# A float32r decoder layer on one core: operand tiles moved to other places in SBUF

## The chip, the cores and the metric

The kernel runs on one core of a Trainium2 chip. The metric is device time in microseconds (us). A program on this core issues work to TensorE (PE, and PEld for its weight loads), VectorE (DVE), ScalarE (ACT), GpSimd (POOL) and SyncE (SP, which here issues the DMAs).

## The reference, cut to what matters

One layer of a decoder for 256 prompt tokens and 8 sample tokens (264 columns in all), in float32:

```
h += 1/2 * rms_post(swiglu_1(rms_pre(h)))            # 2048 -> 2 x 5632 -> 2048
u  = rms_pre(h); proj = u @ w_in                      # 2048 -> 10288
mix = concat(conv_group(proj), ssd_group(proj)) @ w_out
h += rms_post(mix)
h += 1/2 * rms_post(swiglu_2(rms_pre(h)))             # as the first
h += rms_post(sigmoid(rms_pre(h) @ w_ple_gate) * (p @ w_ple_proj))
```

Nearly all arithmetic is in the products with the weight matrices.

## The kernel before, in words

Activations stand with features on the 128 partitions and the 264 tokens along the free dimension. A product with a weight matrix is cut into blocks of 128 x 128 weights; for one block of 128 output features the kernel adds up the blocks of the contraction in one PSUM tile (`acc` or `ps`).

Each float32 product is made of three matmuls in float32r (`mm3`). A weight block is split into a rounded part `hi` and a remainder `lo` (tiles `whi`, `wlo`), and an input tile `act` holds the rounded part of 264 columns (half 0) and the remainder (half 1):

```
nc.tensor.matmul(acc, hi, x[:, 0, :], start=first, stop=False)        # L250
nc.tensor.matmul(acc, hi, x[:, 1, :], start=False, stop=False)        # L251
return nc.tensor.matmul(acc, lo, x[:, 0, :], start=False, stop=last).ins   # L252
```

So L250 and L252 stream half 0 of the input tile past the weights, and L251 streams half 1. Each of the three loads its own 128 x 128 weights.

The weights come in an order written out in a table (`PLAN`). `Weights.load` fetches 8 blocks (512 KB) by a DMA on SP's queue into a tile `wraw` (L153), ACT rounds it into `whi` (L154), DVE subtracts to get `wlo` (L155). Four buffers of each are used in turn. `split` fills an input tile: ACT writes half 0, DVE half 1; 32 buffers `act` are used in turn. `gemm_one` makes one output block, 16 blocks of contraction by three matmuls; `gemm_first` and `gemm_pair` are the same with several output blocks.

Where the tiles lie matters for the change. The built program puts the 32 `act` buffers at byte 23264 of each partition and every 2304 bytes (9 x 256) from there. The four buffers of `wraw` lie from 96992, of `whi` from 113376, of `wlo` from 129760, each 4096 bytes from the last. Counted modulo 256 bytes, half 0 of every `act` tile starts at 224, half 1 (1056 bytes further) at 0, and every block of `whi` and `wlo` at 224. The small tiles (`h`, `tmp`, `y` and so on) lie behind the weight buffers.

`act` tiles are also used twice as plain buffers for DMA: `load_p` reads the input `p` into one (L503), and the projection of `p` is stored from eight of them to `pproj` in HBM (L530), where it is read again near the end.

Of the kernel before, what the change touches and what calls it, by code (L numbers as in the profile page):

```python
# [19 lines left out]
P = 128  # L20
NP_ = 256
NS = 8
T = NP_ + NS
XSTRIDE = 576
DM = 2048
KD = DM // P
FF = 5632
# [100 lines left out]
class Weights:  # L128
# [9 lines left out]
    def load(self, between=()):  # L138

        tc, nc, i = self.tc, self.tc.nc, len(self.done)  # L140
        n = len(PLAN[i][1]) * len(PLAN[i][2])
        src = self.w[i, :, : n * P].rearrange("p (n c) -> p n c", n=n)
        tiles = []
        with nullcontext() if between else tc.high_priority(offset=1000):
            for a in range(0, n, 8):
                if a // 8 < len(between):
                    between[a // 8]()
                m = min(8, n - a)
                raw, hi, lo = (
                    self.pool.tile([P, 8, P], t, tag=tag, bufs=bufs, name=f"{tag}{i}_{a}")[:, :m, :]  # L150
                    for t, tag, bufs in ((F32, "wraw", 4), (F32R, "whi", 4), (F32R, "wlo", 4))
                )
                self.dma = nc.sync.dma_start(raw, src[:, a : a + m, :])  # L153
                nc.scalar.copy(hi, raw)  # L154
                nc.vector.tensor_tensor(out=lo, in0=raw, in1=hi.bitcast(F32), op=ALU.subtract)  # L155
                tiles += [(hi[:, k, :], lo[:, k, :]) for k in range(m)]
        self.done.append(tiles)
# [11 lines left out]
def kernel(ctx: ExitStack, tc: tile.TileContext, a: dict):  # L169
# [13 lines left out]
    uid = [0]  # L183

    def nm(s):
        uid[0] += 1
        return f"{s}_{uid[0]}"
# [7 lines left out]
    def tmp():  # L195
        return apool.tile([P, T], F32, tag="tmp", bufs=6, name=nm("tmp"))

    def act_tile():
        t = xpool.tile([P, XSTRIDE], F32R, tag="act", bufs=32, name=nm("act"))
        return t[:, : 2 * T].rearrange("p (i t) -> p i t", i=2)  # L200

    def ytile():
        return apool.tile([P, T], F32, tag="y", bufs=16, name=nm("y"))
# [4 lines left out]
    def rtile():  # L208
        return apool.tile([P, T], F32, tag="rr", bufs=3, name=nm("rr"))
# [44 lines left out]
    def split(x, gain=None):  # L254

        t = act_tile()
        if gain is None:
            nc.scalar.copy(t[:, 0, :], x)  # L258
            tt(t[:, 1, :], x, t[:, 0, :].bitcast(F32), ALU.subtract)
        else:  # L260
            act(t[:, 0, :], x, AF.Identity, scale=gain)
            stt(t[:, 1, :], x, gain, t[:, 0, :].bitcast(F32), ALU.mult, ALU.subtract)
        return t
# [45 lines left out]
    def rsqrt(out, x, bias=0.0, scale=1.0):  # L309

        act(out, x, AF.Ln, bias=bias, scale=scale)
        act(out, out, AF.Exp, scale=-0.5)

    def rms_scale(p, n):

        r = rtile()
        rsqrt(r, p, eps1, 1.0 / n)
        return r
# [47 lines left out]
    def ffn(xs, sq, done):  # L366
# [5 lines left out]
        def scale(behind):  # L372
            p = sq.total(behind)
            rsqrt(r, p, eps1, 1.0 / DM)
            nc.vector.tensor_scalar(
                out=eq, in0=p, scalar1=EPS / P, scalar2=EPS * EPS * DM / P, op0=ALU.mult, op1=ALU.add
            )
# [42 lines left out]
    def ffn_scale(ysq, eq):  # L420
# [4 lines left out]
        with tc.high_priority():  # L425
            rsqrt(rs, ysq.total(), scale=4.0 / DM)
        return rs
# [73 lines left out]
    def load_p():  # L501
        pt = act_tile().bitcast(F32)
        nc.sync.dma_start(pt, a["p"])  # L503
        pacts.extend(split(pt[:, k, :]) for k in range(2))
# [10 lines left out]
    r = rtile()  # L515
    rsqrt(r, q2, scale=1.0 / DM)


    pproj = dram.tile([P, KD, T], F32, name="pproj")
    for q in range(2):  # L520
        w = ws.next()
        for m in range(8):
            acc = acc_tile()
            mm3(acc, w[m], pacts[0], True, False)
            mm3(acc, w[8 + m], pacts[1], False, True)
            if m % 2 == 0:
                t = act_tile().bitcast(F32)
            nc.scalar.copy(t[:, m % 2, :], acc)
            if m % 2:
                nc.sync.dma_start(pproj[:, 8 * q + m - 1 : 8 * q + m + 1, :], t)  # L530
# [3 lines left out]
    for k in range(KD + 2):  # L534
        if k < KD:
            t = tmp()
            tt(t, ys[k], rs, ALU.mult, nc.gpsimd if k % 2 and k > 2 else nc.vector)
            tt(H(k), H(k), t, ALU.add, nc.gpsimd if k else nc.vector)
        if k >= 2:
            t = tmp()  # L540
# [372 lines left out]
    def update_input(rs, post, pre):  # L913

        xs, sq = [], SumSq(KD, eng=nc.vector)
        for k in range(KD + 2):
            if k < KD:
                with tc.high_priority() if k < 2 else nullcontext():
                    residual(k, ys[k], rs, post)
                    xs.append(split(H(k), V(pre, k)))  # L920
            if k >= 2:
                sq.add(H(k - 2))
        return xs, sq

    with tc.high_priority():
        rs = rms_scale(ysq.total(), DM)
    xs, sq = update_input(rs, "mix_post", "ffn2_pre")
# [48 lines left out]
    for m in range(KD):  # L976
# [6 lines left out]
        t = tmp()  # L983
# [11 lines left out]
    for k in TAIL_TENSOR:  # L995
        p = tps.tile([P, T], F32, tag="sum", bufs=3, name=nm("sum"))
# [22 lines left out]
    for k, n in TAIL_VECTOR:  # L1019
        e, h = pair(e4, k, n), pair(h4, k, n)  # L1020
        on_pe = [i for i in range(k, k + n) if i in TAIL_TENSOR]
        if on_pe:
            tc.keep_in_program_order(tt(e, e, rows(rp, n), ALU.mult))
            for i in on_pe:
                p = sums[TAIL_TENSOR.index(i)]
# [4 lines left out]
        t = tps.tile([P, 2, 512], F32, tag="prod", bufs=1, name=nm("prod"))[:, :n, :T]  # L1030
# [133 lines left out]
```

## Time and profile before

| what | before |
|---|---|
| median of 2 runs | 2432.86 us (2430.39 to 2435.34) |
| the profiled execution: its time | 2432.44 us |
| its span, first to last instruction | 2430.7 us |
| mean granted TensorE clock | 0.993 |
| PE busy | 2367.7 us (97%) |
| DVE, ACT, POOL busy | 1569.2, 1181.4, 298.4 us |
| DMA | 489.89 MB, 202 GB/s in the mean |

The span is 1.7 us shorter than the execution's own time. Busy time of PE counts each matmul from its start to its modelled end, and matmuls overlap; the pace of a stream is therefore read from starts, or from the number of matmuls in a long window. A group's row has the count, the busy time, the mean duration of one in ns, and the idle time ahead of them.

### The profile page before, as it was taken

The page shows a single profiled execution, that of the slowest core. Times are in us where ns is not written, and L with a number is a line of the kernel's source. Part 1 is how long each engine was busy: PE and PEld are TensorE (multiplying, and loading weights), DVE is VectorE, ACT ScalarE, POOL GpSimd, SP SyncE. Part 2 cuts the span into 40 slices and gives each one's busy share as a digit, 9 for nine tenths or more (in the row PEclk, how much of TensorE's full clock was granted, in tenths as well). Part 3 has the DMA queues.
Part 4 walks back from the last instruction along what each step waited for, and adds up shares of the span by engine and source line. Part 5 has one row for each costly group of instructions (what it writes and reads, how often), then busy time and mean ns, then how long its engine had stood idle before and what let it go on. Part 6 is the DMA issues. An engine that isn't in the chain of part 4 may idle for free.

```text
span 2430.7 us, 47409 instructions
## 1 busy us (share of the span) xinstructions
PE 2367.7 (97%) x19448; PEld 2342.7 (96%) x19448; DVE 1569.2 (65%) x2333; ACT 1181.4 (49%) x1771; POOL 298.4 (12%) x295
## 2 busy tenths in 40 slices
PE   8999999999999889999999999999999999999988
PEld 8999999999999889999999999999999999999988
DVE  6554455545557858988798975766545565565585
ACT  6444444433456465665565545544444443344465
POOL 0400000000015212122122010101000000000103
PEclk9999999999999999999999999999999999999999
DMA  7655555555556666666666556476766776676553
GB/s 249 217 183 184 182 183 182 183 183 183 183 169 207 213 180 193 207 216 202 210 216 205 181 181 216 153 238 228 240 213 223 237 236 217 217 236 206 184 191 132
DMA packets 166250, 489.89 MB, mean 202 GB/s; under 512 B 25568, under 2 KB 42640, under 8 KB 166032
## 3 DMA queue, kind: packets, MB, share of 16 engines
q1 hardware_dynamic: 166032, 486.86, 62.0%
q8 instruction: 152, 2.49, 0.4%
q14 instruction: 66, 0.54, 0.1%
HBM read 465.65 MB, written 22.42 MB: 201 GB/s over the span
## 4 chain that ended last, share of the span: by engine, by line
PE 84%; DVE 6%; issue 3%; ACT 3%; DMA 2%; POOL 1%; SPq 0%; ACTq 0%; POOLq 0%; DVEq 0%
PE acc L250 27%; PE acc L251 27%; PE acc L252 27%; DVE wlo L155 2%; DVE y L219 1%; ACT whi L154 1%; PE ps L306 1%; DVE h L216 1%; DMA ab<-d_cs 1%; DMA cbc<-d_bc 1%; DVE ych L794 1%; PE ps L250 0%; ACT tmp L243 0%; DMA d_bc<-rows 0%; PE ps L251 0%
## 5 line engine op out<-in xcount | busy, mean ns | idle before, releaser
L252 PE MATMUL acc<-act,wlo 128*128 128x264 f32 x6224 | 1770.7, 285 | 4.3 <-DVE wlo L155 4.1
L251 PE MATMUL acc<-act,whi 128*128 128x264 f32 x6224 | 1756.6, 283 | 6.3 <-DVE act L216 6.2
L250 PE MATMUL acc<-act,whi 128*128 128x264 f32 x6224 | 1747.7, 283 | 3.4 <-DVE tmp L216 2.1
L155 DVE TENSOR_TENSOR wlo<-wraw,whi 128x1024 fp32r<-128x1024 f32 (+2 forms) x812 | 986.9, 1217 | 597.9 <-ACT whi L154 595.5
L154 ACT CAST whi<-wraw 128x1024 fp32r<-128x1024 f32 (+2 forms) x812 | 829.9, 1026 | 961.9 <-PE acc L251 717.3
L250 PEld LDWEIGHTS acc<-act,whi 128*128 128x128 f32 x6224 | 1175.5, 190 | 6.0 <-issue 2.1
L251 PEld LDWEIGHTS acc<-act,whi 128*128 128x128 f32 x6224 | 1169.2, 188 | 9.9 <-DVE act L216 7.9
L252 PEld LDWEIGHTS acc<-act,wlo 128*128 128x128 f32 x6224 | 1167.9, 188 | 8.3 <-DVE wlo L155 6.4
L216 POOL TENSOR_TENSOR run<-run,tmp 128x264 f32<-128x264 f32 x93 | 87.8, 944 | 962.9 <-ACT tmp L243 961.8
L216 POOL TENSOR_TENSOR s<-s,eap 128x1024 f32<-128x1024 f32 x24 | 48.8, 2035 | 630.4 <-DMA s<-in_hst 630.4
L219 DVE SCALAR_TENSOR_TENSOR y<-v,vec,y 128x251 f32<-128x251 f32 (+23 forms) x240 | 118.1, 512 | 1.2
L219 DVE SCALAR_TENSOR_TENSOR s<-bb,xds,s 128x128 f32<-128x128 f32 x192 | 52.7, 346 | 66.1 <-POOL s L216 66.1
L216 POOL TENSOR_TENSOR h<-h,cbc 128x512 f32<-128x512 f32 x48 | 73.6, 1553 | 166.0 <-DMA cbc<-d_bc 90.9
L258 ACT CAST act<-tmp 128x264 fp32r<-128x264 f32 x120 | 48.7, 410 | 69.9 <-DVE tmp L216 55.2
L216 DVE TENSOR_TENSOR tmp<-acc,rr 128x264 f32<-128x264 f32 x100 | 43.0, 430 | 51.0 <-PE acc L252 50.8
L216 DVE TENSOR_TENSOR tmp<-tmp,acc 128x264 f32<-128x264 f32 x86 | 36.7, 427 | 38.7 <-PE acc L252 38.6
L216 DVE TENSOR_TENSOR act<-tmp,act 128x264 fp32r<-128x264 f32 x120 | 56.1, 471 | 0.3
L243 ACT ACTIVATE tmp<-tmp 128x264 f32<-128x264 f32 x112 | 47.0, 420 | 8.7 <-DVE tmp L216 8.4
L243 ACT ACTIVATE tmp<-y 128x264 f32<-128x264 f32 x67 | 28.0, 425 | 44.1 <-DVE y L216 43.0
L216 DVE TENSOR_TENSOR y<-y,acc 128x264 f32<-128x264 f32 x80 | 34.0, 425 | 24.0 <-PE acc L252 24.0
L794 DVE TENSOR_REDUCE ych<-h 128x4 f32<-128x512 f32 x48 | 32.4, 678 | 17.5 <-POOL h L216 17.5
L250 PE MATMUL ps<-act,whi 128*128 128x264 f32 x96 | 28.4, 304 | 15.4 <-ACT whi L154 8.1
(165 smaller groups left out, 926.1 us busy)
## 6 DMA issues: line engine op xcount, KB each, us to landing
wraw<-in_w SPq DMA_DIRECT2D x756, 512.0 KB, 4.7
h<-in_hst SPq DMA_DIRECT2D x48, 256.0 KB, 3.9
s<-in_hst SPq DMA_DIRECT2D x24, 512.0 KB, 6.5
out_nss<-s SPq DMA_DIRECT2D x24, 512.0 KB, 3.0
wraw<-in_w SPq DMA_DIRECT2D x24, 384.0 KB, 4.1
wraw<-in_w SPq DMA_DIRECT2D x32, 256.0 KB, 3.9
ab<-d_cs SPq DMA_DIRECT2D x16, 384.0 KB, 5.1
cbc<-d_bc SPq DMA_DIRECT2D x8, 512.0 KB, 4.3
```

Of the source, the lines that this page charges most:

```text
L154: nc.scalar.copy(hi, raw)
L155: nc.vector.tensor_tensor(out=lo, in0=raw, in1=hi.bitcast(F32), op=ALU.subtract)
L216: return (eng or nc.vector).tensor_tensor(out=out, in0=in0, in1=in1, op=op)
L219: return nc.vector.scalar_tensor_tensor(out=out, in0=in0, scalar=scalar, in1=in1, op0=op0, op1=op1)
L243: i = nc.scalar.activation(out=out, in_=in_, func=func, bias=bias, scale=scale)
L250: nc.tensor.matmul(acc, hi, x[:, 0, :], start=first, stop=False)
L251: nc.tensor.matmul(acc, hi, x[:, 1, :], start=False, stop=False)
L252: return nc.tensor.matmul(acc, lo, x[:, 0, :], start=False, stop=last).ins
L258: nc.scalar.copy(t[:, 0, :], x)
L306: nc.tensor.matmul(p, ones, s, start=i == 0, stop=i == len(self.parts) - 1)
L794: nc.vector.tensor_reduce(out=ych[:, j, b : b + 4], in_=h0, op=ALU.add, axis=AX.X)
```

## The change

Two things move, and both are addresses alone. Each input tile keeps its buffer of 2304 bytes, but the two halves start at one of 16 pairs of places in it: `lead` elements are left free ahead of half 0, and `gap` elements between the halves (both multiples of 8 elements, 32 bytes). The pair is picked by a running number of the tile's name. And the buffers of `whi` are 16 elements (64 bytes) longer than their contents and those of `wlo` 8 elements (32 bytes), so that the four buffers of each start at different offsets modulo 256 bytes.

```
+PLACES = [(a, b) for a in range(0, 49, 8) for b in range(0, (48 - a) // 2 + 1, 8)]
+WPAD = {"wraw": 0, "whi": 16, "wlo": 8}
...
                 raw, hi, lo = (
-                    self.pool.tile([P, 8, P], t, tag=tag, bufs=bufs, name=f"{tag}{i}_{a}")[:, :m, :]
+                    self.pool.tile(
+                        [P, 8 * P + WPAD[tag]], t, tag=tag, bufs=bufs, name=f"{tag}{i}_{a}"
+                    )[:, : m * P].rearrange("p (m c) -> p m c", c=P)
                     for t, tag, bufs in ((F32, "wraw", 4), (F32R, "whi", 4), (F32R, "wlo", 4))
                 )
...
     def act_tile():
         t = xpool.tile([P, XSTRIDE], F32R, tag="act", bufs=32, name=nm("act"))
-        return t[:, : 2 * T].rearrange("p (i t) -> p i t", i=2)
+        lead, gap = PLACES[uid[0] * 5 % len(PLACES)]
+        n = T + gap
+        return t[:, lead : lead + 2 * n].rearrange("p (i t) -> p i t", i=2)[:, :, :T]
```

In the built program the instructions, their order and their waits are the same on all five engines. The `act` buffers and `wraw` stay where they were; the four buffers of `whi` now start at 224, 32, 96 and 160 modulo 256, those of `wlo` at 224, 0, 32 and 64; every tile behind the weight buffers lies 384 bytes further on. Half 0 and half 1 of the input tiles start at any of the eight multiples of 32 modulo 256. Nine DMAs use an `act` tile as a buffer (one load of `p`, eight stores of `pproj`); where the halves have a gap between them, which is so in the load and in five of the stores, the DMA has two runs of 1056 bytes in each partition in place of one of 2112.

## Prediction

> **What bounds the kernel now.** I read the page's totals first, then the chain of work that ended last, then the groups, then two long windows.
>
> ```profile
> span 2430.7 us, 47409 instructions
> PE 2367.7 (97%) x19448; PEld 2342.7 (96%) x19448; DVE 1569.2 (65%) x2333; ACT 1181.4 (49%) x1771; POOL 298.4 (12%) x295
> PE 84%; DVE 6%; issue 3%; ACT 3%; DMA 2%; POOL 1%; SPq 0%; ACTq 0%; POOLq 0%; DVEq 0%
> ...
> L252 PE MATMUL acc<-act,wlo 128*128 128x264 f32 x6224 | 1770.7, 285 | 4.3 <-DVE wlo L155 4.1
> L251 PE MATMUL acc<-act,whi 128*128 128x264 f32 x6224 | 1756.6, 283 | 6.3 <-DVE act L216 6.2
> L250 PE MATMUL acc<-act,whi 128*128 128x264 f32 x6224 | 1747.7, 283 | 3.4 <-DVE tmp L216 2.1
> L155 DVE TENSOR_TENSOR wlo<-wraw,whi 128x1024 fp32r<-128x1024 f32 (+2 forms) x812 | 986.9, 1217 | 597.9 <-ACT whi L154 595.5
> L154 ACT CAST whi<-wraw 128x1024 fp32r<-128x1024 f32 (+2 forms) x812 | 829.9, 1026 | 961.9 <-PE acc L251 717.3
> ...
> L250 PE MATMUL ps<-act,whi 128*128 128x264 f32 x96 | 28.4, 304 | 15.4 <-ACT whi L154 8.1
> ```
>
> PE is busy for 97% and holds 84% of the chain. The three lines of `mm3` make 3 x (6224 + 96) = 18,960 matmuls, the 96 being those into `ps`. They wait little: idle time ahead of them is a few us each. So what counts is the pace, and two windows show it (the number behind x is the matmuls in the window, PEclk the granted clock).
>
> ```profile
> 100.00:700.00 600.00, 600.00 (x5002) 600.00 (x5001) 306.36 (x333) 246.67 (x299) 9.55 (x19) 1.00 0.58 182
> 1600.00:2300.00 700.00, 700.00 (x5836) 700.00 (x5835) 401.98 (x592) 294.68 (x363) 55.24 (x34) 1.00 0.67 223
> ```
>
> 600 us over 5000 matmuls (two of the 5002 stick out at the edges) are 120.0 ns each, 700 over 5834 again 120.0, at full clock, with POOL nearly idle in the first window and at work in the second. 18,960 x 0.120 = 2275 us, or 94% of the span. The rest, 156 us, is float32 matmuls and stalls at the changes of stage, which this change doesn't touch. **A nanosecond per matmul is worth 19.0 us, 0.8%**; the 2% that a measurement of this kernel can tell from no change is 48.7 us, or 2.6 ns per matmul.
>
> **The places in the trace of before.** The question is whether a matmul's pace depends on where its operands lie. Before has two cases of the streamed operand (half 0 at 224 modulo 256 in L250 and L252, half 1 at 0 in L251) and one of the weights (224). In order of time (start in us, then duration):
>
> ```profile
> 299.82 0.28 PE L250 MATMUL acc<-act,whi 128*128 128x264 f32 x1
> 299.94 0.28 PE L251 MATMUL acc<-act,whi 128*128 128x264 f32 x1
> 300.06 0.28 PE L252 MATMUL acc<-act,wlo 128*128 128x264 f32 x1
> 300.18 0.28 PE L250 MATMUL acc<-act,whi 128*128 128x264 f32 x1
> ...
> 299.83 0.19 PEld L251 LDWEIGHTS acc<-act,whi 128*128 128x128 f32 x1
> 299.95 0.19 PEld L252 LDWEIGHTS acc<-act,wlo 128*128 128x128 f32 x1
> 300.06 0.19 PEld L250 LDWEIGHTS acc<-act,whi 128*128 128x128 f32 x1
> ```
>
> Each step is 0.12 us, and each weight load starts 0 to 0.01 us after the matmul ahead of its own has started. Near the start of the program the same matmuls run in another order, first L250 and L251 by turns, then L252 alone:
>
> ```profile
> 26.91 0.28 PE L250 MATMUL acc<-act,whi 128*128 128x264 f32 x1
> ...
> 27.39 0.28 PE L250 MATMUL acc<-act,whi 128*128 128x264 f32 x1
> 27.52 0.40 PE L252 MATMUL ps<-act,wlo 128*128 128x264 f32 x2
> 27.76 0.64 PE L252 MATMUL acc<-act,wlo 128*128 128x264 f32 x4
> 28.24 0.28 PE L251 MATMUL acc<-act,whi 128*128 128x264 f32 x1
> ```
>
> By turns between 224 and 0, four steps (with the rows left out between) take 27.39 - 26.91 = 0.48 us. With 224 alone, six steps take 28.24 - 27.52 = 0.72. Both are 0.12 per matmul. So the one comparison of places that the trace holds shows no difference at its grain of 10 ns over four to six matmuls, 2 ns each.
>
> Two more things speak of what the pace could be. Float32 matmuls run in two passes of the same 264 columns, each with its own weight load; and short float32 ones of 128 columns exist with operands elsewhere:
>
> ```profile
> 1585.66 0.61 PE L306 MATMUL ps<-run,ones 128*128 128x264 f32 x2
> 1586.11 0.61 PE L306 MATMUL ps<-tmp,ones 128*128 128x264 f32 x2
> ...
> 936.27 0.27 PE L727 MATMUL ps<-ident,h 128*128 128x128 f32 x1
> 936.37 0.27 PE L728 MATMUL ps<-ident,bc 128*128 128x128 f32 x1
> 936.48 0.27 PE L727 MATMUL ps<-ident,h 128*128 128x128 f32 x1
> 936.59 0.27 PE L728 MATMUL ps<-ident,bc 128*128 128x128 f32 x1
> ...
> 890.50 0.72 PE L775 MATMUL ps<-bc,st 128*128 128x128 f32 x5
> 891.06 0.27 PE L781 MATMUL ps<-ident,bc 128*8 128x128 f32 x1
> ```
>
> A pass over 264 columns takes (1586.11 - 1585.66) / 2 = 0.22 us, so a pass at twice the column rate would take 0.111. The short ones take 0.32 / 3 = 0.107 us (weights at 32 and 128 modulo 256, streamed from 192) and 0.56 / 5 = 0.112 us (weights at 64, streamed from 96). All of these load 128 columns of weights each, so a load can be had in 0.107 to 0.112 us from at least these places. The difference of 5 ns is the largest sign of a place in the trace, within its grain, between different instructions.
>
> [...]
>
> **The change part by part.**
>
> *Halves of the input tiles at eight places instead of two.* No instruction comes or goes. Every place is a multiple of 32 bytes, and 1056 bytes from any of them touch the same number of aligned pieces of 16, 32, 64, 128 or 256 bytes as at 224 (33 of 32 bytes, 17 of 64, 5 of 256). And the two reads of PE go at different rates: in each step 1056 bytes stream while 512 are loaded, so their distance sweeps over more than 256 bytes within one matmul, from whatever places they start. I take 0 ns. Ends, by the rows: -9 ns per matmul, if the float32r stream came down to half a two-pass row (0.120 to 0.111), and +10 ns, one step of the slowest that undisturbed steps show below.
>
> *Weight buffers at different places.* The same streams, the other operand; the short rows, with weights at 32, 64 and 128, ask no more than 0.112 us. I take 0 with the same ends, which are not added twice, since it is one pace.
>
> *ACT and DVE write to other places.* They could slow down where they write. The 16 `y` buffers lie 1056 bytes apart and so take all eight places; their additions show how much a place is worth to DVE (min/median/max in ns):
>
> ```profile
> L216 DVE TENSOR_TENSOR y<-y,acc x80: 414/423/431, 479.7 to 2313.7; 128x264 f32<-128x264 f32 x80
> ```
>
> That is 2% from the median at most; on the 1026 and 1217 ns of L154 and L155 it would be 20 to 25 ns per 8 weight blocks, which PE takes 24 x 0.120 = 2.9 us to use. ACT waits 717 us in all for PE to free `whi` ahead of L154; that idle time hides it. Bounds: 0, or, with that cover gone, 812 x 45 ns = 37 us. I take 0, since ACT and DVE have slack in every stage in which PE is dense.
>
> *Six of nine DMAs with two runs in each partition.* The stores and the load, and the first reader of the stores:
>
> ```profile
> L530 SPq DMA_DIRECT2D pproj<-act x8: 319/351/598, 778.0 to 792.5; - x8
> L980 SPq DMA_DIRECT2D e<-pproj x4: 424/425/426, 2353.9 to 2384.1; - x4
> L503 SPq DMA_DIRECT2D act<-in_p x1: 423/423/423, 704.1 to 704.1; - x1
> ```
>
> If a store took twice as long to land (6.4 us in the page's list), its reader is still 1500 us away. An issue on SP of 0.6 us in place of 0.35 delays the weight loads queued behind by 0.25 us each, five times, and the loads run two steps of `PLAN` ahead. The load of `p` is asked for at 704 us and DVE's first reader of it waits in order ahead of the additions into `y`, so a landing later by its own length could hold DVE by some 5 us; PE has buffers for that. Bounds 0 to 6 us; I take 0.
>
> **Sum.** 2430.7 + 0 for the span, 2432.4 for this execution, 0.4 below the median of 2432.86; I give **2433 us**.
>
> **The rivals.** *A small loss of rhythm, +22 us.* In the same program, at the same places, there are stretches in which the stream runs at another rhythm. These rows are the first and the last of 24 steps between them, in a stage with one input tile for several outputs:
>
> ```profile
> 47.37 0.29 PE L250 MATMUL ps<-act,whi 128*128 128x264 f32 x1
> 47.50 0.28 PE L251 MATMUL ps<-act,whi 128*128 128x264 f32 x1
> ...
> 50.28 0.28 PE L250 MATMUL acc<-act,whi 128*128 128x264 f32 x1
> ```
>
> 2.91 / 24 = 0.1212 us, and the first step is 0.13. So the 0.120 is a rhythm into which loads and streams lock, not a floor of either, and changing places might keep it out of lock: 18,960 x 1.2 ns = 22 us, 2455 us. That still counts as no change.
>
> *Colliding reads, slower.* If PE's weight load and its stream hinder each other at some distances modulo 256, before has only two distances (0 and 32 bytes from the next weights), and in the changed program 72% of the matmuls have one of the other six. Priced at 10 ns (a step of 0.13 for one of 0.12) for half of those: 0.36 x 18,960 x 0.010 = 68 us, 2501 us; for all of them 136 us, 2569. It decides from 26% of the matmuls at that price. For it: the rhythm above, and that the pace is 9 ns over half a pass, so something hinders. Against: distances 0 and 32 take the same 0.120, and the sweep.
>
> *Colliding reads, freed.* The same mechanism the other way: what holds the pace at 0.120 is that stream and weights start at the same place, and mixed places free it. All 18,960 at 0.111 would give 2432 - 171 = 2262 us; a third of them 2432 - 57 = 2376. It decides from 28%. Against it: L251 streams from another place than the weights and keeps the same 0.120.
>
> [...] That other engines don't disturb PE the two windows bear out; that the two reads don't disturb each other no row here shows.
>
> **How the numbers follow.** No change 0.50, loss of rhythm 0.12, together 0.62 within 2%; slower by collisions 0.22; faster 0.16. The likeliest case's own range is 2420 to 2455. To hold 8 in 10 the range goes up to half of the collisions (2501, taken as 2504 with the DMA's few us) and down to a third of the freed (2376). Left out are about half of the slower case and most of the faster one.
>
> **What would show it.** In the profile of the changed kernel, 5000 matmuls in 100 to 700 us and 5834 in 1600 to 2300 would bear out the forecast; 4950 the loss of rhythm; 4850 or fewer the collision, with single steps of 0.13 that come back with the same input tile, since each tile has one place for a whole stage; above 5100 the freed reads. The mean of L154 and L155 and PE's idle time ahead of L252 would show a loss on the writing engines. I am wrong if the pace itself depends on a place that before never used, for which the trace has no row.

## The result and the profile after

| what | before | after |
|---|---|---|
| median | 2432.86 us | 2457.11 us (2455.81 to 2458.40, 2 runs) |
| ratio to before, 95% interval | | 1.0103 [1.0084, 1.0123] |
| the profiled execution: time, span | 2432.44, 2430.7 us | 2458.40, 2456.7 us |

The changed kernel is 1.0% slower: clear of noise, and within the 2% that was called no change. Its totals and its costliest groups (the lines of the kernel are 5 or 7 further down: L257 to L259 are the matmuls of `mm3`, L159 and L160 the writers of `whi` and `wlo`):

```profile
span 2456.7 us, 47409 instructions
PE 2398.6 (98%) x19448; PEld 2374.6 (97%) x19448; DVE 1574.7 (64%) x2333; ACT 1180.9 (48%) x1771; POOL 300.3 (12%) x295
...
DMA packets 167018, 489.89 MB, mean 199 GB/s; under 512 B 25568, under 2 KB 44176, under 8 KB 166800
...
L258 PE MATMUL acc<-act,whi 128*128 128x264 f32 x6224 | 1776.1, 286 | 6.2 <-DVE act L223 6.1
L259 PE MATMUL acc<-act,wlo 128*128 128x264 f32 x6224 | 1771.4, 285 | 2.1 <-DVE wlo L160 2.1
L257 PE MATMUL acc<-act,whi 128*128 128x264 f32 x6224 | 1767.7, 286 | 3.0 <-DVE tmp L223 2.0
L160 DVE TENSOR_TENSOR wlo<-wraw,whi 128x1024 fp32r<-128x1024 f32 (+2 forms) x812 | 992.5, 1224 | 620.5 <-ACT whi L159 615.1
L159 ACT CAST whi<-wraw 128x1024 fp32r<-128x1024 f32 (+2 forms) x812 | 828.9, 1024 | 1010.2 <-PE acc L258 729.2
```

PE waits no more than before for its operands (11.3 us of idle time ahead of the three lines, 14.0 before), the writers take as long as before (1024 and 1224 ns against 1026 and 1217), and the split DMAs show as some 770 more packets and in no wait of PE. What changed is the pace, in the same windows as before:

```profile
100.00:700.00 600.00, 600.00 (x4926) 600.00 (x4926) 301.23 (x328) 241.96 (x292) 13.08 (x26) 1.00 0.57 181
700.00:800.00 100.00, 99.78 (x808) 99.17 (x806) 67.22 (x89) 63.84 (x114) 40.11 (x49) 1.00 0.59 187
...
1600.00:2300.00 700.00, 699.59 (x5726) 699.34 (x5725) 401.58 (x589) 287.97 (x355) 52.82 (x30) 1.00 0.67 220
```

4924 and 5724 matmuls are 121.9 and 122.3 ns each, against 120.0, at the same full clock. All steps from one matmul's start to the next of up to 200 ns sum up to 2309.5 us after and 2273.9 before, 35.6 more (18 more steps fall into this group after, which is 2 us of it). The longer steps (the stalls at the changes of stage, the float32 passes over 264 columns at 0.22 us, and the stretches at a granted clock of 0.50, such as 863.0 to 865.5 us before, where a step takes 0.22 us) sum up to 129.9 us after and 140.0 before. So in these two executions the stream lost 36 us and the longer steps gave 10 back, which makes the 26 us between the two spans. That they give back because the stream is slower isn't shown: a later run at the old pace of 120.0 ns (all inputs and `wlo` moved by 64 bytes, below) has 135.7 us of them, so some 4 of the 10 can be a difference between executions. One place of giving back is the window 700 to 800 us, of which this is the row before:

```profile
700.00:800.00 100.00, 96.01 (x763) 94.16 (x762) 73.09 (x96) 63.90 (x118) 48.67 (x57) 0.98 0.64 207
```

The stage there ends later in the changed kernel, so only a part of this can be read from one window; the sums over all steps are what the 10 us rest on.

The pace of a single matmul now depends on which tiles it reads, and repeats. The same input tile with the same weight buffer, two output blocks apart (start, duration):

```profile
101.16 0.29 PE L257 MATMUL acc<-act,whi 128*128 128x264 f32 x1
101.29 0.29 PE L258 MATMUL acc<-act,whi 128*128 128x264 f32 x1
101.42 0.28 PE L259 MATMUL acc<-act,wlo 128*128 128x264 f32 x1
...
112.85 0.29 PE L257 MATMUL acc<-act,whi 128*128 128x264 f32 x1
112.98 0.29 PE L258 MATMUL acc<-act,whi 128*128 128x264 f32 x1
113.11 0.28 PE L259 MATMUL acc<-act,wlo 128*128 128x264 f32 x1
```

Both times two steps of 0.13. Over 100 to 290 us the groups of three matmuls spread from 355 to 376 ns with a standard deviation of 3.3 ns, and by about 1 ns among groups with the same tile and block. It is no noise, and no waiting for another engine: ahead of these matmuls PE has 0.0 us of idle time in that stretch.

### The profile page after: what moved, and what is told of

It reads as the page before. It is cut to its first block, busy times and chain, and to the rows that moved or that the text cites. A ratio compares the mean times of both kernels' runs of the same rounds, so it can differ in the third digit from the quotient of the medians.

```text
span 2456.7 us, 47409 instructions
## 1 busy us (share of the span) xinstructions
PE 2398.6 (98%) x19448; PEld 2374.6 (97%) x19448; DVE 1574.7 (64%) x2333; ACT 1180.9 (48%) x1771; POOL 300.3 (12%) x295
## 4 chain that ended last, share of the span: by engine, by line
PE 55%; DVE 4%; DMA 2%; issue 1%; ACT 1%; POOL 1%; SPq 0%; ACTq 0%; POOLq 0%; DVEq 0%
PE acc L257 17%; PE acc L258 17%; PE acc L259 17%; DVE wlo L160 1%; DMA h<-in_hst 1%; DVE y L226 1%; DMA ab<-d_cs 1%; POOL run L223 0%; PE ps L313 0%; PE ps L775 0%; DVE h L223 0%; DMA d_bc<-rows 0%; PE ps L257 0%; ACT whi L159 0%; POOL h L223 0%
## 5 line engine op out<-in xcount | busy, mean ns | idle before, releaser
L258 PE MATMUL acc<-act,whi 128*128 128x264 f32 x6224 | 1776.1, 286 | 6.2 <-DVE act L223 6.1
L259 PE MATMUL acc<-act,wlo 128*128 128x264 f32 x6224 | 1771.4, 285 | 2.1 <-DVE wlo L160 2.1
L257 PE MATMUL acc<-act,whi 128*128 128x264 f32 x6224 | 1767.7, 286 | 3.0 <-DVE tmp L223 2.0
L160 DVE TENSOR_TENSOR wlo<-wraw,whi 128x1024 fp32r<-128x1024 f32 (+2 forms) x812 | 992.5, 1224 | 620.5 <-ACT whi L159 615.1
L159 ACT CAST whi<-wraw 128x1024 fp32r<-128x1024 f32 (+2 forms) x812 | 828.9, 1024 | 1010.2 <-PE acc L258 729.2
L259 PEld LDWEIGHTS acc<-act,wlo 128*128 128x128 f32 x6224 | 1175.1, 189 | 5.3 <-DVE wlo L160 3.4
L257 PEld LDWEIGHTS acc<-act,whi 128*128 128x128 f32 x6224 | 1172.3, 189 | 5.6 <-issue 2.1
L250 ACT ACTIVATE tmp<-tmp 128x264 f32<-128x264 f32 x112 | 46.8, 419 | 7.5 <-DVE tmp L223 7.2
L250 ACT ACTIVATE tmp<-y 128x264 f32<-128x264 f32 x67 | 28.0, 425 | 42.9 <-DVE y L223 41.8
L257 PE MATMUL ps<-act,whi 128*128 128x264 f32 x96 | 29.0, 311 | 16.8 <-ACT whi L159 9.4
```

Of the source, the lines that this page charges most:

```text
L250: i = nc.scalar.activation(out=out, in_=in_, func=func, bias=bias, scale=scale)
```

## The experiments

Paces below are read from windows as above (two or three of the matmuls in a window's count stick out at its edges) or, in the short windows and where two decimals are given, are means over the groups of three in a stage, from the starts in the trace. Code cuts with a comment give an edit in short.

**The two halves of the change.** In the first run `WPAD` is zero, in the second `PLACES` isn't used.

```
-WPAD = {"wraw": 0, "whi": 16, "wlo": 8}
+WPAD = {"wraw": 0, "whi": 0, "wlo": 0}
```

> Only the input tiles move (the 16 pairs of places by turns); the weight buffers stay at 224 modulo 256. Theory 1, rhythm: what costs is that the places change from one block to the next, no place is bad by itself. Then this half carries nearly all of the loss: about 121.5 to 122 ns per matmul in the dense windows, 4920 to 4940 matmuls in 100 to 700 us, 2448 to 2457 us in all. Theory 2, distances: certain distances modulo 256 between the stream and the weights cost, and before has only the free ones (0 and 32). Then it costs in proportion to the matmuls at other distances, about as much as the whole change too, 2450 to 2457 us. Theory 3, the writers or the DMAs: ACT, DVE or the split DMAs are slower and PE waits; then the dense windows stay at 120.0.

```
-        lead, gap = PLACES[uid[0] * 5 % len(PLACES)]
+        lead, gap = 0, 0
```

> Only the weight buffers move (four buffers at four offsets each); the input tiles stay at 224 and 0. Within a run of 24 matmuls nothing changes but between hi and lo. Theory 1, rhythm: nearly free, 120.0 to 120.4 ns per matmul, 2432 to 2440 us. Theory 2, distances: three of four buffers stand at distances that before never had, so it costs nearly as much as the inputs do, 2448 us or more. If both halves cost in full and don't add, it is neither rhythm of single blocks nor a sum of places.

The window 100 to 700 us, inputs alone:

```profile
100.00:700.00 600.00, 600.00 (x4931) 600.00 (x4930) 300.84 (x327) 242.72 (x293) 11.51 (x25) 1.00 0.57 180
```

and weights alone:

```profile
100.00:700.00 600.00, 600.00 (x4957) 600.00 (x4956) 302.64 (x330) 243.22 (x294) 11.85 (x25) 1.00 0.56 181
```

Inputs alone: 2451.12 us, 1.0092 [1.0073, 1.0111], 121.7 ns. Weights alone: 2447.03 us, 1.0061 [1.0043, 1.0080], 121.1 ns. The second is not nearly free, as theory 1 had it, though nothing but hi and lo changes for 24 matmuls on end. And the two halves don't add up: 0.9% and 0.6% make 1.0% together. The trace of weights alone has a sign for theory 2: with four buffers of eight blocks the groups of three repeat every 32, and seven in a row of each 32 take exactly 360 ns, while the others lie between 358 and 370. Only one of the four pairs of buffers stands at the distances of the kernel before.

**One place for a whole stage.** `act_tile` takes its place from a variable that each stage sets once.

```
-        lead, gap = PLACES[uid[0] * 5 % len(PLACES)]
+        lead, gap = place[0]      # set once ahead of each stage
```

> Weights at 224 as before; all input tiles of a stage share one place, another in each stage: half 0 moved by 32 to 192 bytes, or a gap of 32 to 96 bytes between the halves. Theory 1, rhythm: whatever the place, each dense stage runs at a steady 120.0 ns per matmul, every group of three repeats to the nanosecond, 2433 us in all. Theory 2, distances: the stages differ, some at 120.0, others at 122 or more, each steady by itself. A stage below 119 would show a place that is better than the one of before.

In the next one `wlo` has a pool of its own behind 16 elements of padding, with the same places of the inputs.

> As the run with one place per stage, and all wlo buffers moved by 64 bytes against whi (224 and 32 modulo 256), the same in every buffer. Theory 1: still 120.0 in each dense stage. Theory 2: other paces than in that run at the same input places. Together the two runs give some 18 fixed pairings of stream and weights; a pace below 119 in one of them would be a version to build.

Two windows of the first, with the input tiles moved by 64 bytes and by nothing:

```profile
200.00:290.00 90.00, 90.00 (x745) 90.00 (x744) 38.33 (x32) 36.98 (x48) 0.00 (x0) 1.00 0.56 182
...
1850.00:2000.00 150.00, 150.00 (x1252) 150.00 (x1252) 92.51 (x139) 63.30 (x79) 13.59 (x7) 1.00 0.71 239
```

and one of the run with `wlo` moved, at the same inputs as the first row:

```profile
200.00:290.00 90.00, 90.00 (x753) 90.00 (x752) 39.05 (x33) 36.67 (x46) 0.00 (x0) 1.00 0.57 184
```

The two windows of 90 us run at 121.11 and 120.00 ns, the one of 150 us at 120.00. With a single place for a whole stage most stages ran at 120.7 to 122.3 ns; theory 1, by which any steady place is free, fell here. No stage of either run was faster than 120.0 in the mean. With `wlo` moved, two pairs of input places ran at exactly 120.00 (254 of 255 groups, and 256 of 256, took 360 ns), a third at 120.00 in the mean (groups of 356 and 364 ns), others at up to 122.8. The first run took 2444.73 us, 1.0061 [1.0040, 1.0081], the one with `wlo` moved 2438.8 us in one execution.

**The same distances at other addresses.** Both weight buffers move by 64 bytes, or by 32, and the inputs of each stage so that distances come again.

```
+    hpad, lpad = ...              # 16 (or 8) elements ahead of the whi buffers
```

> All weight buffers moved by 64 bytes (32 modulo 256), and the input tiles of each stage at one place, chosen so that many pairs of distances (half 0 from whi, half 1 from wlo) come again that earlier runs had at other addresses: (0, 32) as in the kernel before, for 100 to 290 us; (32, 64), (64, 96), (96, 128), (0, 64), (0, 96), (192, 224). Theory 2, narrowed to distances alone: each pair has the pace that it had there: 120.0, 121.3, 121.1, 121.7, 121.3, 121.5, 120.8 ns. If the address itself counts, paces differ between runs at the same distances, and (0, 32) needn't be 120.0. In either case no pace under 120.0.

> As the run moved by 64, with the weights moved by 32 bytes (0 modulo 256). Distances alone: (0, 32) at 120.0 in 100 to 290 us and the other pairs as listed there. If what counts is the start modulo 64, this run (streams and weights at other halves of 64 bytes) differs from the kernel before at the same distances, and the run moved by 64 does not.

Moved by 64, the first row at the distances of the kernel before, the second at (32, 64):

```profile
100.00:190.00 90.00, 90.00 (x752) 90.00 (x751) 47.71 (x55) 37.97 (x48) 10.37 (x22) 1.00 0.57 184
200.00:290.00 90.00, 90.00 (x744) 90.00 (x743) 37.99 (x31) 36.70 (x46) 0.00 (x0) 1.00 0.55 182
```

Moved by 32, the same two pairs:

```profile
100.00:190.00 90.00, 90.00 (x753) 90.00 (x752) 47.76 (x55) 38.35 (x48) 10.86 (x23) 1.00 0.57 183
200.00:290.00 90.00, 90.00 (x745) 90.00 (x744) 38.16 (x33) 36.70 (x46) 0.00 (x0) 1.00 0.57 181
```

The paces in ns, by distance (bytes modulo 256 from `whi` to half 0 and from `wlo` to half 1, with `whi` and `wlo` at the same offset):

| distances | weights at 224 | moved by 64 | moved by 32 |
|---|---|---|---|
| 0, 32 | 120.0 | 120.0 | 120.0 |
| 32, 64 | 121.28 | 121.27 | 121.27 |
| 64, 96 | 121.12 | 121.11 | 121.11 |
| 96, 128 | 121.66 | 121.70 | 121.72 |
| 128, 160 | 122.25 | 122.23 | 122.27 |
| 160, 192 | 122.22 | | 122.22 |
| 192, 224 | 120.77 | 120.00, later 120.74 | |
| 224, 0 | | 122.20 | 122.20 |
| 0, 64 | 121.33 | 121.32 | 121.34 |
| 0, 96 | 121.49 | 121.49 | 121.49 |

The first run took 2437.15 us, the second 2446.22, each in one execution. Theory 2, narrowed to distances: nearly every pair has the same pace wherever it lies, to 0.06 ns. The row (192, 224) shows what distances don't settle. With the weights moved by 64, the same input tiles at the same distances ran at 120.00 in 1600 to 1730 us and at 120.74 in 1850 to 2000 us, with other tiles in between:

```profile
1600.00:1730.00 130.00, 130.00 (x1085) 130.00 (x1085) 80.22 (x124) 55.80 (x70) 10.18 (x5) 1.00 0.71 238
...
1850.00:2000.00 150.00, 150.00 (x1245) 150.00 (x1244) 92.81 (x148) 63.13 (x78) 12.62 (x7) 1.00 0.70 234
```

The kernel before does the same, at (0, 32): a stall at 1359 us is followed by some 80 us at 121.1 ns, at full clock, in place of 120.0. A window in it:

```profile
1375.00:1425.00 50.00, 50.00 (x415) 50.00 (x414) 49.36 (x94) 19.76 (x24) 1.44 (x2) 1.00 0.59 191
```

So one pair of distances can run in more than one steady rhythm, 0.7 to 1.1 ns apart, and what puts it into one or the other no run here shows. Distances 128 apart aren't alike (120.0 at (0, 32), 122.25 at (128, 160)), while the buffers differ by all multiples of 256 (the inputs) and of 512 (the weight blocks) within a stage of steady 120.0, so here the period is 256 bytes. Two distances aren't the whole of it: with `wlo` moved against `whi` the pair (0, 64) ran at 122.2 in place of 121.33.

**Does change itself cost?** With `wlo` moved by 64, input tiles by turns at the two pairs of places that each ran at 120.00.

```
+        turn[0] += 1
-        lead, gap = PLACES[uid[0] * 5 % len(PLACES)]
+        lead, gap = [(16, 0), (0, 16)][turn[0] % 2]
```

> whi at 224, wlo at 32 modulo 256; input tiles by turns at two pairs of places, (32, 64) and (224, 64), each of which alone ran at 120.00 ns per matmul in the run with wlo moved. If the loss belongs to the places, turns between two good ones stay at 120.0, 5000 matmuls in 100 to 700 us, and about 2430 us. If the change from block to block itself costs (theory 1), the pace is 121 or more, 4960 or fewer, 2445 us or more.

```profile
100.00:700.00 600.00, 600.00 (x4956) 600.00 (x4956) 302.69 (x329) 243.96 (x294) 11.25 (x24) 1.00 0.56 181
```

In this window 121.1 ns; 2447.32 us, 1.0076 [1.0049, 1.0104]. So turns between two good places cost, too: what theory 1 has from the change itself is real, beside what the distances cost. The price isn't one number. Up to 1740 us the run keeps to 121.11, and from 1750 us on, in the same turns, to 122.22 (1227 matmuls in 150 us):

```profile
1850.00:2000.00 150.00, 150.00 (x1229) 150.00 (x1229) 91.61 (x138) 62.13 (x78) 11.96 (x7) 1.00 0.70 236
```

How much of the changed kernel's 1.9 ns comes from turns and how much from distances, no run separates.

**Whole kernels by distance.** Two predictions from the paces so far. All inputs at `lead` 40, weights as before; then all inputs at `lead` 16 with `wlo` moved by 64.

```
-        lead, gap = PLACES[uid[0] * 5 % len(PLACES)]
+        lead, gap = 40, 0         # or 16, 0, and wlo 64 bytes further on
```

> Weights as before; every input tile at one and the same place, 160 bytes further on: half 0 stands 160 from whi, half 1 192 from wlo, nothing changes from block to block. By distances: that pair ran at 122.2 ns per matmul at two other addresses, so 2.2 x 18,960 = 42 us more in the stream, less some 8 us that the longer steps gave back after the change: 2460 to 2472 us, slower than the changed kernel itself though no place ever changes. If only changing places cost: 2433.

> All input tiles 64 bytes further on and all wlo buffers 64 bytes further on: other places for three of four kinds of read, at a pair of distances (64 from whi, 32 from wlo) that ran at 120.00. By distances: no difference to the kernel before within 0.4%, 5000 matmuls in 100 to 700 us.

Distances (160, 192):

```profile
100.00:700.00 600.00, 600.00 (x4911) 600.00 (x4910) 300.25 (x327) 241.08 (x291) 10.93 (x21) 1.00 0.56 180
```

Inputs and `wlo` moved by 64:

```profile
100.00:700.00 600.00, 600.00 (x5003) 600.00 (x5002) 306.10 (x333) 246.59 (x299) 10.11 (x21) 1.00 0.57 183
```

The first: 122.2 ns, 2460.67 us, 1.0124 [1.0109, 1.0139], at the lower end of what was expected, and slower than the changed kernel in their medians (the intervals overlap), with no place that ever changes. The second: 120.0 ns, 2428.30 us, 0.9993 [0.9984, 1.0003]; as fast as the kernel before, at other places. That is the version that the experiments pointed to, and it is no faster.

**Smaller steps.** One place per stage again, moved by 4, 8, 16 bytes and the like.

> Input tiles of each stage moved by 4, 8, 16, 24 or 176 bytes in place of multiples of 32, or with a gap of 4 to 16 bytes between the halves; weights as before. If distances count in pieces of 32 bytes or more, moves of 4 to 16 bytes keep the 120.0 of the kernel before; if they count by the byte, each stage has its own pace between 120.0 and 123. A pace below 119.5 anywhere would break the reading of 120.0 as a floor and be a version to build.

```profile
100.00:190.00 90.00, 90.00 (x726) 90.00 (x725) 45.88 (x53) 36.52 (x46) 12.18 (x23) 1.00 0.55 177
200.00:290.00 90.00, 90.00 (x732) 90.00 (x731) 37.63 (x33) 36.10 (x46) 0.00 (x0) 1.00 0.56 177
...
1850.00:2000.00 150.00, 150.00 (x1252) 150.00 (x1252) 90.61 (x139) 63.41 (x79) 12.96 (x6) 1.00 0.70 232
2025.00:2105.00 80.00, 80.00 (x669) 80.00 (x668) 44.08 (x60) 30.07 (x30) 3.82 (x3) 1.00 0.66 219
```

Both halves moved by 4 bytes: 124.4 ns; by 8: 123.3. Half 1 alone moved by 4 (third row): 120.0. Both by 16, half 1 by another 16 (fourth row): 120.0. Both by 16 alone is at 120.0 as well, half 1 alone by 16 at 121.1, and half 0 by 24 with half 1 by 40 at 123.0. So moves smaller than 32 bytes change the pace, and the three places with half 0 moved by 4, 8 and 24 bytes (124.4, 123.3, 123.0 ns) cost more than any of the pairs in the table. That it is half 0 that costs there is inferred from half 1 alone being free at 4 and 8 bytes; half 0 alone was not moved. Again nothing is below 120.0. The run took 2453.11 us, one execution.

**What the 120.0 is.** Two runs that leave out work: the correction matmuls over 192 columns, then all three over 192 but for the first block of a contraction.

```
-        nc.tensor.matmul(acc, hi, x[:, 1, :], start=False, stop=False)
+        nc.tensor.matmul(acc[:, :192], hi, x[:, 1, :192], start=False, stop=False)
```

> Addresses as before; the two correction matmuls of each product (the half 1 stream and the lo weights) run over 192 of the 264 columns, so the last 72 columns lack their corrections. If the stream of columns sets the floor, two of three matmuls shorten by up to 72 columns, 30 ns, and the pace goes to about 100 ns. If the chain of weight loads sets it, each load starting when the matmul ahead of its own has started, the pace stays at 120.0, or changes by a ns or two with the rhythm; with loads at the 0.107 to 0.112 us of the short float32 rows it would be 110 to 112 for those two.

> Addresses as before; all three matmuls of a product run over 192 of the 264 columns, but for the first block of a contraction, so the last 72 columns lack 15 of 16 blocks of their sums or so. A stream of 192 columns alone would take 80 ns at the rate of half a two-pass row. If the load is the floor and the stream only gets in its way, the pace comes down to that of the short float32 rows, 107 to 112 ns, and no lower, although the stream would allow 80; if the floor of 120.0 were a fixed cost of a load, it stays at 120; if stream and load simply add up, near 114 less another 8 ns.

Corrections over 192 columns, the window and three steps:

```profile
100.00:700.00 600.00, 600.00 (x5243) 600.00 (x5243) 325.43 (x361) 265.40 (x331) 20.27 (x31) 1.00 0.59 191
...
300.10 0.30 PE L250 MATMUL acc<-act,whi 128*128 128x264 f32 x1
300.25 0.25 PE L251 MATMUL acc<-act,whi 128*128 128x192 f32 x1
300.33 0.27 PE L252 MATMUL acc<-act,wlo 128*128 128x192 f32 x1
300.44 0.31 PE L250 MATMUL acc<-act,whi 128*128 128x264 f32 x1
```

All over 192:

```profile
301.17 0.27 PE L251 MATMUL acc<-act,whi 128*128 128x192 f32 x1
...
302.17 0.28 PE L251 MATMUL acc<-act,whi 128*128 128x192 f32 x1
```

In the first the mean is 114.5 ns, neither the 100 of a bound by columns (an estimate: 120.0 less 30 ns in two of three matmuls, 30 ns being 72 columns at half a two-pass row's 0.222 us for 264) nor a fixed 120. In the second nine steps take 1.00 us, 0.111 each, where a bound by columns would allow 0.080, an estimate from the same half a two-pass row: that is about the pace of the short float32 rows (0.107 to 0.112), which load the same 128 columns of weights. My reading is that with the short stream the weight load is the bound, at 111 ns; another cost per matmul that doesn't depend on its columns would look the same. The extra 9 to 12 ns of the full kernel come with a stream of 264 columns, which alone would take about as long as the load, by the same estimate (0.111). That the two reads get in each other's way there, by their distance modulo 256 and by the rhythm they are in, fits all runs. How they do so no run here shows. The two runs took 2367.08 and 2331.74 us, one execution each.

## Why the prediction was right or wrong

The time, 2457.1, lies in the range, and within 2% as forecast. It is 24 us over the number, 2 us above the likeliest case's own range, and 2 us from the rival "a small loss of rhythm" (2455). So the likeliest case was not what happened. That the time still falls within the 2% is luck as far as that case goes: its 0 ns was 1.9, and 2.6 would have left the 2%.

- *The pace, the unit of account* (120.0 ns, 19.0 us for a nanosecond): right. 1.9 ns in 36 us of stream, and it decided everything.
- **The step that failed** is "halves of the input tiles at eight places: I take 0 ns". The table shows up to 2.3 ns for one place kept up, and the changed kernel's window 1.9. Two of its reasons fell. Equal counts of aligned pieces don't make equal paces: the places in the table are all multiples of 32 bytes, and run at 120.0 to 122.3 ns. And the sweep, by which the start would not matter, is contradicted by the constant distances of the run at (160, 192), 1.2% slower.
- *The comparison of places in the trace of before.* L250 and L252 against L251 took the same 0.12, and I took that as a sign that places don't matter. But all of them belonged to one rhythm at the pair (0, 32), which happens to be one of the few at the floor. The row told nothing of other pairs; the last sentence of the prediction, that the trace has no row for them, was the better reading of it.
- *Weight buffers, not added twice*: right that it is one pace and that the halves don't add; wrong that it is 0 (1.0061 alone).
- *The rhythm rival*: right in size, from a stretch of the kernel before that ran at 0.1212. Its reason, that changing places cost, is half of it: turns between two good places cost 1.1 ns in one stretch and 2.2 in another, and steady bad distances up to 2.3. Its premise, that 0.120 is a rhythm that the stream can fall out of at the same places, the two paces at (0, 32) and at (192, 224) bear out.
- *The collision rival*: that the pace goes by distances modulo 256 the runs bear out (120.0 at (0, 32), 122.2 at (160, 192)); that load and stream hinder each other fits them and isn't shown; its price wasn't borne out. 10 ns was read from a step of 0.13, but such a step is followed by shorter ones, and steady pairs cost 0 to 2.8 ns at multiples of 32 bytes. Its sign, single steps of 0.13 that come back with the same tile, is there, but it doesn't tell the two rivals apart: the turns between two good places show it, too (in 1850 to 2000 us a step of 131 ns comes back in every second group). What tells them apart is the run at the constant distances (160, 192).
- *The freed rival*: nothing went below 120.0 in the mean at 264 columns in any of some 30 pairings.
- *ACT, DVE and the DMAs at 0*: right, by the rows above.
- *Left out*: the steps over 200 ns, which were 10 us shorter against the stream's 36 more. Why they were is open; some 4 us can be a difference between executions.

## What to carry to other kernels

In this kernel, with dense streams of 264 columns against loads of 128 (120 ns a matmul; short rows with the same loads 107 to 112), where the operands lie was worth 1.2% of the whole time, and up to 2.3% of the pace of a stage at multiples of 32 bytes. In a kernel like it: keep all input tiles and weight buffers at constant offsets modulo 256 bytes, try a few distances between the two, and read the pace from the number of matmuls in a long dense window, which shows a tenth of a nanosecond in a single profile. In the stream of before, whose groups repeat at 360 ns, the comparison between L250, L251 and L252 showed the same 0.12 and told nothing of the 122.2 ns at other places; nor does one stretch settle a place, since the same place ran at 120.00 in one and at 121.1 in another. In the one run that tried them, starts of half 0 moved by 4, 8 and 24 bytes were the slowest of all (124.4, 123.3 and 123.0 ns).

## What the runs showed of the hardware that was not expected

- The pace of the dense stream depends on the distances between operands modulo 256 bytes: 120.0 at (0, 32), 122.2 at (160, 192), the same at other addresses to 0.06 ns.
- It doesn't depend on them alone. At the same distances, in one run, the stream keeps to 120.00 for one stretch and to 121.1 for another (the kernel before), or to 120.00 and 120.74 (weights moved by 64).
- Steady inputs gave a rhythm longer than a group of three: at (0, 64) groups of 365, 362, 354, 371 and 368 ns came 48 to 53 times each.
- Both halves moved by 8 and by 4 bytes cost 3.3 and 4.4 ns, half 1 alone nothing (120.03 at 4, 120.07 at 8).
- Loads of 128 columns with 192-column streams beside them ran at 111 ns; with one matmul in three over 264 columns the mean is 114.5, and the step from the long one to the next takes 0.144 us.
